# Two-layer hybrid decoder trunk on one core: the mixer's input and output projections as plain fp32 products instead of three split products

## The chip, the cores and the metric

The kernel runs on one core of one Trainium2 chip. The metric is the device time of one execution in microseconds (us); lower is better. The engines named below are TensorE (PE, with its weight loads listed apart as PEld), VectorE (DVE), ScalarE (ACT), GpSimd (POOL) and SyncE (SP), which only issues transfers.

## The reference

The input is one sequence of 256 tokens with 1024 channels. Each of two layers is FFN, mixer, FFN, every one of them behind a modulated LayerNorm and followed by a residual LayerNorm. Cut to what matters:

```python
for l in range(2):
    x = norm(ALPHA * x + 0.5 * gate * swiglu(modulate(x), w_gate, w_up, w_down))   # 1024 -> 2816 -> 1024
    h = modulate(x)
    z = h @ w_in[l]                                   # 1024 -> 2048
    q, k, v, u_ssm, u_pool = split(z, 512, 512, 512, 256, 256)
    y = concat(dilated_attention(q, k, v),            # 8 heads x 64, three branches
               s5(u_ssm),                             # 16 groups, 64 complex states each, scan, GLU
               pool_mixer(u_pool))                    # trailing means of 2, 4, 8, 16
    x = norm(ALPHA * x + gate * (y @ w_out[l]))       # 1024 -> 1024
    x = norm(ALPHA * x + 0.5 * gate * swiglu(modulate(x), ...))
```

All of it is in fp32.

## The kernel before

The 256 tokens are two tiles of 128, called tt 0 and tt 1. Weights come from memory in pieces of 128 x 1024 (512 KB). `process` (L368) loads a piece into a slot called `raw`; for the pieces of the four matrices (`gu` and `wd` of the FFN, `win` and `wout` of the mixer) ACT copies it to `hi` in the type fp32r (L379) and DVE takes the rest, `lo = raw - hi` (L380). So a piece lives on in two slots of the 41 that there are for everything of this size (`N_W`). The other operand is split in the same way: `HT` holds the transposed modulated tokens as hi and lo halves (`parts`, L502).

A product of two split numbers is then three fp32r matmuls, x_hi w_hi, x_lo w_hi and x_hi w_lo. `linear` (L535) does it for the FFN's first matrix and for the mixer's input projection: for each of 8 slices kt of 128 input channels, the three matmuls L544, L545 and L546, each 128x512. The input projection has four parts of 512 columns, named B (the channels of SSM and pooling), V, Q and K; their results are `pB`, `pV`, `pQ`, `pK`. `project` (L549) does it for the FFN's last matrix and the output projection, with two column halves, so six matmuls for each kt (L556, L561); the mixer's accumulators are `dm`.

Inside `mixer` (L822) the steps are written in the list `MIXER_ORDER`. `ssm jj tt` is a chain through a PE product (`pbu`, L914), DVE multiplications (L927, L929), additions on POOL or DVE (L932), scans on DVE (L939), and a PE product into `py` (L950). `scores tt` makes the logits on PE in `psc` (L969), DVE adds the bias into `lg` (L975), DVE takes maxima, ACT the exponentials; `attend` turns the probabilities on PE (`ppt`, L993) and multiplies with V (`po`, L1004). Scores of tt 1 are made in two sets of heads, and the first bank of the second set is the first bank of the first one (`SCORE_BANKS`). `glu` and `pooling` end the other two branches. All three write their results into `HT` again, as hi and lo, each through one ACT and one DVE instruction (L508 and L509, L1033 and L1034, L1072 and L1073). `out` (L1077) multiplies them with `wout`, first tt 0, then tt 1. `chain` (L511) is the residual sum and the two LayerNorms, on DVE almost alone (from `y`, L522, to `z`, L471); the transposes of `z` on PE are `pn` (L475), and ACT makes the modulated `h` (L481).

The order on each engine is not that in which the code is written: every step is recorded with its engine and a written cost, and `Plan.order` (L134) places the steps one after the other by those costs, by slot and bank, and by rank in the program. A step's cost of 0.695 is given for the three matmuls of `linear`. So a change of costs or of steps gives another order on all five engines.

Of the kernel before, what the change touches and what calls it, by code (L numbers as in the profile page):

```python
# [21 lines left out]
NU = DFF // 256  # L22
# [28 lines left out]
WAIT = {"DVE": 0.25, "ACT": 0.25, "Pool": 1.3}  # L51
BUFS = {"w": N_W, "th": 2, "a": 2, "aT": 2, "st": 3, "carry": 1, "a3": 1, "gu": 2, "t": 2, "d0": 1, "d1": 1, "d2": 1, "d3": 1}
# [212 lines left out]
class Build:  # L265
    def __init__(self, tc, io, pools):
        self.tc, self.nc, self.io, self.pools = tc, tc.nc, io, pools
        self.plan = Plan()
        self.items, self.next = [], 0
        self.ready, self.acc, self.bc = {}, {}, {}  # L270
        self.exd, self.turns = [], []
# [96 lines left out]
    def process(self):  # L368

        nc = self.nc  # L370
        x = self.items[self.next]
        self.next += 1
        t = self.slot("raw")
        self.load(lambda: nc.sync.dma_start(out=t[:], in_=self.src(x)), [], [t], 0.5)
        if x[0] == "ada" and x[3] == 0:
            self.start_sum(*x[1:3])
        if x[0] in ("gu", "wd", "win", "wout"):
            hi, lo = self.slot("hi", F32R), self.slot("lo", F32R)
            self.act(1024, lambda: nc.scalar.copy(out=hi[:], in_=t[:]), [t], [hi])  # L379
# [77 lines left out]
    def modulated(self, tt, l, sub):  # L457

        for h, pt in enumerate(self.normed(tt, ("t", "t"))):
            hs = self.slot("h") if h == 0 else hs  # L460
            for k in range(4 * h, 4 * h + 4):
                self.shifted(hs, pt, k, tt, l, sub)
            self.parts(lambda h=h, hs=hs: hs[:, h * 512:(h + 1) * 512].rearrange("p (k t) -> p k t", k=4), [(hs, 4 * h + b) for b in range(4)], 4 * h, 4, tt)
# [20 lines left out]
    def first(self):  # L484

        pts = [list(self.normed(tt, ("t", "t") if tt == 0 else ("d2", "d3"))) for tt in range(2)]
        hs = [self.slot("h") for _ in range(2)]
        for k in range(8):
# [46 lines left out]
    def linear(self, out, tt, pieces):  # L535

        nc = self.nc
        for kt in range(8):
            hi, lo = self.need(pieces[kt // 2])
# [7 lines left out]
            self.pe(0.695, go, [hi, lo] + [(self.HT, (p, kt, tt)) for p in range(2)], [out])  # L547

# [41 lines left out]
    def unit(self, l, sub, f, tt, u, d):  # L590
# [9 lines left out]
        t = self.buf("aT", [128, 2, 2, 128], F32R)  # L600
        self.act(256, lambda: nc.scalar.copy(out=t[:, 0], in_=pt[:]), [pt], [(t, 0)])  # L601
        self.dve(256, lambda: nc.vector.tensor_tensor(out=t[:, 1], in0=pt[:], in1=t[:, 0].bitcast(F32), op=ALU.subtract), [pt, (t, 0)], [(t, 1)])  # L602

        def down():
            for kk in range(2):
                w = self.need(("wd", l, f, u, kk))
                self.project(d, lambda kk=kk: t[:, 0, kk, :], lambda kk=kk: t[:, 1, kk, :], [t], w, u == 0 and kk == 0, u == NU - 1 and kk == 1)
# [214 lines left out]
    def mixer(self, l):  # L822
# [17 lines left out]

        V = lambda: made["v"][:].rearrange("p (s c) -> p s c", s=2)
# [145 lines left out]
        def attend(tt):  # L987
# [20 lines left out]
            self.turned(lambda k: qf()[:, tt, k * 128:(k + 1) * 128], [(place("qf"), ("f", tt))], 4, 0, tt)  # L1008

        def glu(tt):  # L1010
# [20 lines left out]
            self.dve(256, lambda: nc.vector.scalar_tensor_tensor(out=z[:], in0=z[:], scalar=1.0, in1=yv[:], op0=ALU.add, op1=ALU.mult), [z, yv], [z])  # L1031
            kh, kl = [[(HT, (p, kt, tt)) for kt in (4, 5)] for p in range(2)]
# [6 lines left out]
        def pooling(tt):  # L1039
# [29 lines left out]
            for j in range(2):  # L1069
                o = O_PS + l * 2 + j  # L1070
                kh, kl = [[(HT, (p, 6 + j, tt))] for p in range(2)]
                self.act(128, lambda j=j, o=o: nc.scalar.activation(out=HT[:, 0, 6 + j, c], in_=pz[:, j, :], func=AF.Copy, scale=sm[:, o:o + 1]), [pz, sm], kh, 0.1)  # L1072
                self.dve(128, lambda j=j, o=o: nc.vector.scalar_tensor_tensor(out=HT[:, 1, 6 + j, c], in0=pz[:, j, :], scalar=sm[:, o:o + 1],  # L1073
# [3 lines left out]
        def out(tt):  # L1077
            d = [self.bank(f"d{2 * tt + h}", name=f"dm{tt}{h}") for h in range(2)]
            for kt in WOUT:
                xh, xl = (lambda i=i, kt=kt: HT[:, i, kt, cols[tt]] for i in range(2))  # L1080
# [25 lines left out]
def build(tc, io):  # L1106
    with tc.tile_pool(name="sb", bufs=1) as sb, tc.tile_pool(name="ps", bufs=1, space=bass.MemoryType.PSUM) as ps, \
            tc.tile_pool(name="dram", bufs=1, space=bass.MemoryType.DRAM) as dram:
        with tc.manual_schedule():
            Build(tc, io, dict(sb=sb, ps=ps, dram=dram)).run()  # L1110

# [89 lines left out]
```

## Time and profile before

| what | value |
|---|---|
| device time, median of 3 | 1108.52 us (1105.32 to 1110.19) |
| the profiled execution, device time | 1107.35 us |
| its span, from the first instruction to the last | 1105.6 us |
| PE busy | 1026.4 us (93%) |
| DVE busy | 864.6 us (78%) |
| ACT busy | 501.0 us (45%) |
| POOL busy | 300.3 us (27%) |
| mean granted TensorE clock | 0.975 of full speed |

Matmuls are pipelined, so the time of one is read from start to start and not from its length; the busy share says only how long no gap stood between them. The first mixer lies at about 236 to 366 us, the second at about 772 to 895 us, and the four FFNs around them.

### The profile page before, as it was taken

How to read it: one execution, taken by the hardware profiler on the slowest of the kernel's cores; microseconds unless marked ns; L12 is line 12 of the kernel's file. 1: busy time of each engine (PE TensorE's matmuls, PEld its weight loads, DVE VectorE, ACT ScalarE, POOL GpSimd, SP SyncE). 2: the span in 40 equal slices, each digit the busy share in tenths (PEclk: the TensorE clock that was granted, in tenths of full speed). 3: DMA queues.
4: the chain of work that ended last, by engine and by line, in shares of the span. 5: the costliest groups of instructions: out<-in, count | busy, mean ns of one | idle time of the engine just before them, and what ended most of it. 6: DMA issues, size and time to landing. Idle time of an engine off the chain costs nothing. (4 is left out here: it accounts for less than half of the span.)

```text
span 1105.6 us, 13448 instructions
## 1 busy us (share of the span) xinstructions
PE 1026.4 (93%) x4626; PEld 802.6 (73%) x4626; DVE 864.6 (78%) x1254; ACT 501.0 (45%) x799; POOL 300.3 (27%) x449
## 2 busy tenths in 40 slices
PE   4899999979989799999999999999997989999996
PEld 3578877657767577788876887778775767887885
DVE  7978877998899899845389988758987999755423
ACT  3764444253356635434274544415425665544400
POOL 2057758023751100088610000001485010000000
PEclk9899999998998899999999999999998999999998
DMA  9988889984635489946486998968563447765601
GB/s 357 408 340 298 298 300 340 341 307 166 192 115 172 175 309 351 321 131 222 170 299 217 382 342 300 315 207 286 184 220 131 153 171 261 257 204 161 199 3 38
DMA packets 73551, 266.49 MB, mean 241 GB/s; under 512 B 8307, under 2 KB 8443, under 8 KB 73484
## 3 DMA queue, kind: packets, MB, share of 16 engines
q1 hardware_dynamic: 68556, 248.15, 63.5%
q0 software_dynamic: 4928, 17.50, 4.6%
q8 instruction: 36, 0.59, 0.2%
q14 instruction: 31, 0.25, 0.1%
HBM read 258.00 MB, written 7.61 MB: 240 GB/s over the span
## 5 line engine op out<-in xcount | busy, mean ns | idle before, releaser
L379 ACT CAST hi<-raw 128x1024 fp32r<-128x1024 f32 x312 | 323.0, 1052 | 205.2 <-DMA raw<-in_gu_dram 92.6
L380 DVE TENSOR_TENSOR lo<-raw,hi 128x1024 fp32r<-128x1024 f32 x312 | 379.7, 1237 | 42.0 <-ACT hi L379 38.2
L544 PE MATMUL gu<-hi,HT 128*128 128x512 f32 x704 | 291.2, 414 | 10.2 <-ACT hi L379 5.6
L546 PE MATMUL gu<-lo,HT 128*128 128x512 f32 x704 | 281.4, 400 | 8.5 <-DVE lo L380 8.5
L545 PE MATMUL gu<-hi,HT 128*128 128x512 f32 x704 | 283.7, 403 | 0.7 <-DVE HT L509 0.7
L556 PE MATMUL d<-hi,aT 128*128 128x512 f32 x672 | 183.5, 394 | 1.9 <-ACT aT L601 1.7
L546 PEld LDWEIGHTS gu<-lo,HT 128*128 128x128 f32 x704 | 134.2, 191 | 46.6 <-DVE lo L380 14.5
L544 PEld LDWEIGHTS gu<-hi,HT 128*128 128x128 f32 x704 | 134.4, 191 | 42.6 <-ACT hi L379 7.9
L545 PEld LDWEIGHTS gu<-hi,HT 128*128 128x128 f32 x704 | 134.8, 192 | 29.7 <-DVE HT L509 1.6
L556 PEld LDWEIGHTS d<-hi,aT 128*128 128x128 f32 x672 | 125.1, 188 | 33.4 <-ACT aT L601 3.6
L441 POOL TENSOR_TENSOR st<-st,power 128x1 f32<-128x1 f32 x24 | 27.9, 1160 | 385.6 <-DVE st L440 385.6
L388 DVE CUSTOM_DVE_ANT_0 raw<-raw,row,sm 128x1024 f32<-128x1024 f32 x96 | 123.3, 1295 | 3.6 <-DMA raw<-in_at_dram 3.6
L597 DVE TENSOR_TENSOR a<-th,gu 128x256 f32<-128x256 f32 x88 | 36.8, 419 | 99.4 <-ACT th L596 99.2
L596 ACT ACTIVATE th<-gu 128x256 f32<-128x256 f32 x88 | 33.7, 383 | 177.1 <-PE gu L546 176.9
L556 PE MATMUL d<-lo,aT 128*128 128x512 f32 x336 | 104.7, 393 | 0.0
L556 PEld LDWEIGHTS d<-lo,aT 128*128 128x128 f32 x336 | 63.1, 188 | 13.9
L932 POOL TENSOR_TENSOR w<-w 128x256 f32<-128x256 f32 x57 | 53.0, 945 | 50.8 <-DVE w L929 27.7
L395 DVE SCALAR_TENSOR_TENSOR acc<-raw,cond,acc 128x1024 f32<-128x1024 f32 x48 | 63.1, 1315 | 1.3 <-DMA raw<-in_ada_dram 1.3
L602 DVE TENSOR_TENSOR aT<-pa,aT 128x256 fp32r<-128x256 f32 x88 | 37.1, 421 | 33.8 <-ACT aT L601 33.1
L601 ACT CAST aT<-pa 128x256 fp32r<-128x256 f32 x88 | 32.9, 373 | 56.8 <-PE pa L599 56.5
L481 ACT ACTIVATE h<-pn,mod 128x128 f32<-128x128 f32 x96 | 36.8, 466 | 44.8 <-PE pn L475 24.9
L828 POOL DMA_DIRECT2D ex<-exd x2 | 1.1, 561 | 166.2 <-DMA raw<-in_gb_dram 149.5
(206 smaller groups left out, 1219.7 us busy)
## 6 DMA issues: line engine op xcount, KB each, us to landing
raw<-in_gu_dram SPq DMA_DIRECT2D x176, 512.0 KB, 5.3
raw<-in_at_dram SPq DMA_DIRECT2D x96, 512.0 KB, 6.2
raw<-in_wd_dram SPq DMA_DIRECT2D x88, 512.0 KB, 5.6
raw<-in_ada_dram SPq DMA_DIRECT2D x48, 512.0 KB, 5.3
raw<-in_win_dram SPq DMA_DIRECT2D x32, 512.0 KB, 6.3
raw<-in_wout_dram SPq DMA_DIRECT2D x16, 512.0 KB, 4.2
raw<-in_gb_dram SPq DMA_DIRECT2D x12, 512.0 KB, 5.5
lg<-biasd POOLq DMA_DIRECT2D x6, 512.0 KB, 5.8
```

Of the source, the lines that this page charges most:

```text
L379: self.act(1024, lambda: nc.scalar.copy(out=hi[:], in_=t[:]), [t], [hi])
L380: self.dve(1024, lambda: nc.vector.tensor_tensor(out=lo[:], in0=t[:], in1=hi[:].bitcast(F32), op=ALU.subtract), [t, hi], [lo])
L388: self.dve(1090, lambda: nc.vector.tensor_tensor_reduce(out=t[:], in0=t[:], in1=self.row[:], scale=1.0, scalar=self.sm[:, O_ADA + k:O_ADA ...
L395: self.dve(1090, lambda: nc.vector.scalar_tensor_tensor(out=acc[:], in0=t[:], scalar=self.cond[:, q:q + 1], in1=acc[:], op0=ALU.mult, op1= ...
L481: self.act(128, lambda: self.nc.scalar.activation(out=hs[:, k * 128:(k + 1) * 128], in_=pt[:, k % 4, :], func=AF.Identity, scale=sc(), bia ...
L544: nc.tensor.matmul(out[:], xh, hi[:, c], start=kt == 0, stop=False)
L545: nc.tensor.matmul(out[:], xl, hi[:, c], start=False, stop=False)
L546: nc.tensor.matmul(out[:], xh, lo[:, c], start=False, stop=kt == 7)
L556: nc.tensor.matmul(d[h][:], a(), b[:, c[h]], start=start, stop=stop)
L597: self.dve(256, lambda: nc.vector.tensor_tensor(out=a[:], in0=th[:], in1=ps[:, 256:512], op=ALU.mult), [th, ps], [a])
L602: self.dve(256, lambda: nc.vector.tensor_tensor(out=t[:, 1], in0=pt[:], in1=t[:, 0].bitcast(F32), op=ALU.subtract), [pt, (t, 0)], [(t, 1)])
L932: self.either(256, lambda eng, r=r, op=op: eng.tensor_tensor(out=x()[:, :, r, :], in0=x()[:, :, r, :], in1=y()[:, :, r, :], op=op), [kx, k ...
```

## The change

The names in `WHOLE` tell which products are made whole. For all four parts of `win` and for `wout`, a piece is no longer split: the slot `raw` itself is an operand. `linear` takes for these the unsplit `h` (kept in `self.hs`) and one fp32 matmul per kt; `out` takes a new slot `o0` or `o1`, into which attention, GLU and pooling write their results unsplit by ACT, and two fp32 matmuls per kt (`whole_product`). `WHOLE_UNITS` is empty, so the FFNs keep their split products, and `modulated` still splits `h` into `HT` ahead of the mixer too.

```diff
+WHOLE = ("B", "V", "Q", "K", "O")
+WHOLE_UNITS = ()
...
-        if x[0] in ("gu", "wd", "win", "wout"):
+        if whole(x):
+            self.ready[x] = t
+        elif x[0] in ("gu", "wd", "win", "wout"):
             hi, lo = self.slot("hi", F32R), self.slot("lo", F32R)
...
         for kt in range(8):
+            if whole(pieces[kt // 2]):
+                w, hs = self.need(pieces[kt // 2]), self.hs[tt]
+                self.pe(0.86, lambda kt=kt, w=w, hs=hs: nc.tensor.matmul(
+                    out[:], hs[:, kt * 128:(kt + 1) * 128], w[:, kt % 2 * 512:kt % 2 * 512 + 512], start=kt == 0, stop=kt == 7), [w, (hs, kt)], [out])
+                continue
             hi, lo = self.need(pieces[kt // 2])
...
+    def whole_product(self, d, x, key, w, first, last):
+        for h in range(2):
+            self.pe(0.86, lambda h=h: self.nc.tensor.matmul(d[h][:], x(), w[:, h * 512:(h + 1) * 512], start=first, stop=last), key + [w], [d[h]])
...
+        mix = lambda tt: made[f"o{tt}"][:].rearrange("p (k t) -> p k t", k=8)
...
-            self.turned(lambda k: qf()[:, tt, k * 128:(k + 1) * 128], [(place("qf"), ("f", tt))], 4, 0, tt)
+            if whole(("wout", l, 0)):
+                turn(lambda: qf()[:, tt, :], [(place("qf"), ("f", tt))], [lambda: mix(tt)[:, 0:4, :]], [(place(f"o{tt}"), 0)])
...
+            if whole(("wout", l, 4)):
+                self.act(256, lambda: nc.scalar.activation(out=mix(tt)[:, 4:6, :], in_=z[:], func=AF.Copy, scale=0.5), [z], [(place(f"o{tt}"), 1)])
+                return
...
+                if whole(("wout", l, 6)):
+                    self.act(128, lambda j=j, i=i: nc.scalar.activation(out=mix(tt)[:, 6 + j, :], in_=pz[:, j, :], func=AF.Copy, scale=sm[:, i:i + 1]),
+                             [pz, sm], [(place(f"o{tt}"), 2)], 0.1)
+                    continue
...
             for kt in WOUT:
+                if whole(("wout", l, kt)):
+                    w = self.need(("wout", l, kt))
+                    self.whole_product(d, lambda kt=kt: mix(tt)[:, kt, :], [(place(f"o{tt}"), 0 if kt < 4 else kt // 2 - 1)], w, kt == WOUT[0], kt == WOUT[-1])
+                    continue
...
+def whole(x):
+
+    return x[0] == "win" and x[2] in WHOLE or x[0] == "wout" and "O" in WHOLE or x[0] in ("gu", "wd") and x[3] in WHOLE_UNITS
```

The order moves on every engine. Line numbers of the changed kernel are a few to thirty higher (L547 is the whole product of `linear`, L562 that of `out`, L888 and L893 the turn and its copy, L938 `pbu`, L480 `pn`). First, PE at the start of the first mixer, where tt 0 is ready and tt 1 is still in `chain`. Before:

```order
L544 MATMUL pB_2134<-hi_2004,HT 128x512
L545 MATMUL pB_2134<-hi_2004,HT 128x512
L546 MATMUL pB_2134<-lo_2181,HT 128x512
L544 MATMUL pB_2134<-hi_2004,HT 128x512
L545 MATMUL pB_2134<-hi_2004,HT 128x512
L546 MATMUL pB_2134<-lo_2181,HT 128x512
L475 MATMUL pn_2195<-ident,z_2187 128x128 x4
L475 MATMUL pn_2201<-ident,z_2187 128x128 x4
L544 MATMUL pB_2134<-hi_2024,HT 128x512
```

In the changed kernel, from the first product of the mixer:

```order
L547 MATMUL pB_2113<-raw_1937,h_2107 128x512 x2
L547 MATMUL pB_2113<-raw_1958,h_2107 128x512 x2
L547 MATMUL pB_2113<-raw_1982,h_2107 128x512 x2
L547 MATMUL pB_2113<-raw_1991,h_2107 128x512 x2
L547 MATMUL pV_2151<-raw_2037,h_2107 128x512
L888 MATMUL ptr_2158<-ident,bt_2153 128x128 x4
L547 MATMUL pV_2151<-raw_2037,h_2107 128x512
L938 MATMUL pbu_2170<-uu_2164,ex_1877 128x128 x4
L547 MATMUL pV_2151<-raw_2051,h_2107 128x512 x2
L547 MATMUL pV_2151<-raw_2077,h_2107 128x512 x2
L547 MATMUL pV_2151<-raw_2090,h_2107 128x512
L480 MATMUL pn_2200<-ident,z_2197 128x128 x4
```

Before, 18 matmuls of `pB` stand ahead of the transposes of tt 1; now all 8 products of B and 7 of V do, with the first SSM product among them.

Second, DVE in the first mixer, at the scores of tt 1, of which `psc_2841` (before) and `psc_2645` (now) are the first set's first bank. Before:

```order
L939 SCALAR_TENSOR_TENSOR w_367_2804<-rad,carry_2333,w_367_2804 128x128
L939 SCALAR_TENSOR_TENSOR w_369_2742<-rad,carry_2333,w_369_2742 128x128
L927 TENSOR_TENSOR w_368_2876<-w_367_2804,cos_2456 128x512
L929 TENSOR_TENSOR w_368_2876<-w_367_2804,sin_2474 128x2x128
L939 SCALAR_TENSOR_TENSOR w_369_2742<-rad,carry_2333,w_369_2742 128x128
L929 TENSOR_TENSOR w_368_2876<-w_367_2804,sin_2474 128x2x128
L927 TENSOR_TENSOR w_370_2881<-w_369_2742,cos_2456 128x512
L975 TENSOR_TENSOR lg_2318<-psc_2841,lg_2318 128x2x256
```

In the changed kernel:

```order
L951 TENSOR_TENSOR w_338_2609<-pbu_2589,cos_2246 128x512
L1058 SCALAR_TENSOR_TENSOR z_2623<-z_2623,yv_2448 128x256
L956 TENSOR_TENSOR w_334_2618<-w_334_2618 128x2x128
L999 TENSOR_TENSOR lg_2098<-psc_2645,lg_2098 128x2x256
L963 SCALAR_TENSOR_TENSOR w_336_2595<-rad,carry_2233,w_336_2595 128x128
L963 SCALAR_TENSOR_TENSOR w_338_2609<-rad,carry_2233,w_338_2609 128x128
```

Before, the addition into `lg` that frees the bank stands behind the scans (L939) of the last two SSM steps; now it stands ahead of them (L963).

Third, PE at the end of the first mixer, where `out` of tt 1 goes over into the next FFN. Before:

```order
L561 MATMUL dm_7_3084<-lo_3022,HT 128x512
L561 MATMUL dm_3_3085<-hi_2829,HT 128x512 x2
L561 MATMUL dm_3_3085<-lo_3022,HT 128x512
L475 MATMUL pn_3183<-ident,z_3180 128x128 x4
L475 MATMUL pn_3191<-ident,z_3180 128x128 x4
L544 MATMUL gu_3215<-hi_2993,HT 128x512
```

In the changed kernel:

```order
L480 MATMUL pn_2902<-ident,z_2896 128x128 x4
L480 MATMUL pn_2909<-ident,z_2896 128x128 x4
L562 MATMUL dm_3_2852<-raw_2385,o_342_2832 128x512
L562 MATMUL dm_7_2846<-raw_2395,o_342_2832 128x512
L562 MATMUL dm_3_2852<-raw_2395,o_342_2832 128x512
L555 MATMUL gu_2935<-hi_2585,HT 128x512
```

Before, the transposes of tt 0 stand behind the last output product; now three products stand between them and the FFN's first matmul. The second and the third place read alike in the changed kernel's second mixer.

## Rows read from the trace of the kernel before

**Rows 1.** The page: span, busy time and share of PE.

```profile
span 1105.6 us, 13448 instructions
...
PE 1026.4 (93%) x4626; PEld 802.6 (73%) x4626; DVE 864.6 (78%) x1254; ACT 501.0 (45%) x799; POOL 300.3 (27%) x449
```

**Rows 2.** Waits of PE, first mixer: who waited for whom, sum, times, longest.

```profile
PE pB L546 <- DVE lo L380: 6.8, 1, 6.8
PE psc L969 <- DVE lg L975: 5.5, 1, 5.5
PE pB L544 <- ACT HT L508: 1.3, 1, 1.3
```

**Rows 3.** Waits of PE, 355 to 385 us: first mixer into FFN.

```profile
PE gu L546 <- DVE lo L380: 2.5, 1, 2.5
PE gu L544 <- ACT HT L508: 2.0, 1, 2.0
```

**Rows 4.** Waits of PE, second mixer.

```profile
PE psc L969 <- DVE lg L975: 3.0, 1, 3.0
PE ppt L993 <- ACT k L869: 1.7, 1, 1.7
```

**Rows 5.** Waits of PE, 895 to 920 us: second mixer into FFN.

```profile
PE gu L544 <- ACT HT L508: 2.1, 1, 2.1
PE pn L475 <- DVE z L471: 1.3, 1, 1.3
```

**Rows 6.** Windows: stretch, length, busy time of each engine, granted clock, DMA.

```profile
250.00:256.00 6.00, 6.00 (x18) 5.05 (x19) 5.16 (x7) 3.08 (x9) 0.31 (x1) 0.50 0.00 0
333.00:337.00 4.00, 4.00 (x23) 2.88 (x24) 4.00 (x8) 1.74 (x6) 1.57 (x2) 0.50 0.54 178
378.00:386.00 8.00, 7.26 (x23) 5.26 (x24) 7.74 (x11) 6.38 (x15) 0.22 (x1) 0.57 0.21 67
844.00:852.00 8.00, 7.80 (x40) 5.85 (x40) 6.92 (x14) 2.99 (x5) 2.51 (x3) 0.63 0.56 187
856.00:860.00 4.00, 3.08 (x14) 2.16 (x15) 4.00 (x10) 0.42 (x1) 1.44 (x2) 0.60 0.22 50
902.00:905.00 3.00, 3.00 (x9) 2.32 (x9) 2.85 (x3) 1.33 (x2) 0.00 (x0) 0.57 0.33 86
```

**Rows 7.** Timeline of PE, one split product to the next: start, length.

```profile
264.80 0.40 PE L544 MATMUL pV<-hi,HT 128*128 128x512 f32 x1
...
265.50 0.40 PE L544 MATMUL pV<-hi,HT 128*128 128x512 f32 x1
```

**Rows 8.** Timeline and source line of L724 (two plain fp32 products per row).

```profile
76.25 1.88 PE L724 MATMUL pflip<-rev,onehot 128*128 128x512 f32 x4
...
L724 PE MATMUL pflip<-rev,onehot x8: 592/593/697, 76.3 to 80.7; 128*128 128x512 f32 x8
```

**Rows 9.** The page's groups of the two splitting lines.

```profile
L379 ACT CAST hi<-raw 128x1024 fp32r<-128x1024 f32 x312 | 323.0, 1052 | 205.2 <-DMA raw<-in_gu_dram 92.6
L380 DVE TENSOR_TENSOR lo<-raw,hi 128x1024 fp32r<-128x1024 f32 x312 | 379.7, 1237 | 42.0 <-ACT hi L379 38.2
```

**Rows 10.** Windows of L380 alone on DVE: length, busy time, clock, DMA.

```profile
262.00:312.00 50.00, 11.93 (x9) 1.00 0.62 208
312.00:338.00 26.00, 0.00 (x0) 0.87 0.37 122
835.00:862.00 27.00, 0.00 (x0) 0.81 0.40 134
```

**Rows 11.** Timeline of DVE, `chain` from `y` to `z`: tt 1, then tt 0.

```profile
238.07 0.68 DVE L522 SCALAR_TENSOR_TENSOR y<-d,bc 128x512 f32<-128x512 f32 x1
...
250.34 1.00 DVE L471 TENSOR_SCALAR z<-X,st 128x512 f32<-128x512 f32 x2 [0.45 <-POOL st L441]
...
353.51 1.39 DVE L522 SCALAR_TENSOR_TENSOR y<-dm,bc 128x512 f32<-128x512 f32 x2 [0.59 <-PE dm L561]
...
366.20 0.99 DVE L471 TENSOR_SCALAR z<-X,st 128x512 f32<-128x512 f32 x2
```

More of the change, by code (lines that the diff above doesn't have):

```diff
@@ L269, in __init__ @@
         self.items, self.next = [], 0
-        self.ready, self.acc, self.bc = {}, {}, {}
+        self.ready, self.acc, self.bc, self.hs = {}, {}, {}, [None, None]
         self.exd, self.turns = [], []
@@ L459, in modulated @@
         for h, pt in enumerate(self.normed(tt, ("t", "t"))):
-            hs = self.slot("h") if h == 0 else hs
+            if h == 0:
+                hs = self.hs[tt] = self.slot("h")
             for k in range(4 * h, 4 * h + 4):
@@ L487, in first @@
         hs = [self.slot("h") for _ in range(2)]
+        self.hs = list(hs)
         for k in range(8):
@@ L599, in unit @@
         self.pe(0.22, lambda: [nc.tensor.transpose(pt[:, b, :], a[:, b * 128:(b + 1) * 128], self.ident[:]) for b in range(2)], [a, self.ident], [pt])
-        t = self.buf("aT", [128, 2, 2, 128], F32R)
-        self.act(256, lambda: nc.scalar.copy(out=t[:, 0], in_=pt[:]), [pt], [(t, 0)])
-        self.dve(256, lambda: nc.vector.tensor_tensor(out=t[:, 1], in0=pt[:], in1=t[:, 0].bitcast(F32), op=ALU.subtract), [pt, (t, 0)], [(t, 1)])
+        if whole(("wd", l, f, u, 0)):
+            t = self.buf("aT", [128, 2, 128])
+            self.act(256, lambda: nc.scalar.copy(out=t[:], in_=pt[:]), [pt], [t])
+        else:
+            t = self.buf("aT", [128, 2, 2, 128], F32R)
+            self.act(256, lambda: nc.scalar.copy(out=t[:, 0], in_=pt[:]), [pt], [(t, 0)])
+            self.dve(256, lambda: nc.vector.tensor_tensor(out=t[:, 1], in0=pt[:], in1=t[:, 0].bitcast(F32), op=ALU.subtract), [pt, (t, 0)], [(t, 1)])
         def down():
@@ L606, in down @@
                 w = self.need(("wd", l, f, u, kk))
-                self.project(d, lambda kk=kk: t[:, 0, kk, :], lambda kk=kk: t[:, 1, kk, :], [t], w, u == 0 and kk == 0, u == NU - 1 and kk == 1)
+                first, last = u == 0 and kk == 0, u == NU - 1 and kk == 1
+                if whole(("wd", l, f, u, kk)):
+                    self.whole_product(d, lambda kk=kk: t[:, kk, :], [t], w, first, last)
+                else:
+                    self.project(d, lambda kk=kk: t[:, 0, kk, :], lambda kk=kk: t[:, 1, kk, :], [t], w, first, last)
         return down
@@ L1007, in attend @@
                      [p, (dn, (0, tt))], [(place("qf"), ("f", tt))])
-            self.turned(lambda k: qf()[:, tt, k * 128:(k + 1) * 128], [(place("qf"), ("f", tt))], 4, 0, tt)
+            if whole(("wout", l, 0)):
+                turn(lambda: qf()[:, tt, :], [(place("qf"), ("f", tt))], [lambda: mix(tt)[:, 0:4, :]], [(place(f"o{tt}"), 0)])
+            else:
+                self.turned(lambda k: qf()[:, tt, k * 128:(k + 1) * 128], [(place("qf"), ("f", tt))], 4, 0, tt)
         def glu(tt):
@@ L1069, in pooling @@
             for j in range(2):
-                o = O_PS + l * 2 + j
+                i = O_PS + l * 2 + j
+                if whole(("wout", l, 6)):
+                    self.act(128, lambda j=j, i=i: nc.scalar.activation(out=mix(tt)[:, 6 + j, :], in_=pz[:, j, :], func=AF.Copy, scale=sm[:, i:i + 1]),
+                             [pz, sm], [(place(f"o{tt}"), 2)], 0.1)
+                    continue
                 kh, kl = [[(HT, (p, 6 + j, tt))] for p in range(2)]
-                self.act(128, lambda j=j, o=o: nc.scalar.activation(out=HT[:, 0, 6 + j, c], in_=pz[:, j, :], func=AF.Copy, scale=sm[:, o:o + 1]), [pz, sm], kh, 0.1)
-                self.dve(128, lambda j=j, o=o: nc.vector.scalar_tensor_tensor(out=HT[:, 1, 6 + j, c], in0=pz[:, j, :], scalar=sm[:, o:o + 1],
+                self.act(128, lambda j=j, i=i: nc.scalar.activation(out=HT[:, 0, 6 + j, c], in_=pz[:, j, :], func=AF.Copy, scale=sm[:, i:i + 1]), [pz, sm], kh, 0.1)
+                self.dve(128, lambda j=j, i=i: nc.vector.scalar_tensor_tensor(out=HT[:, 1, 6 + j, c], in0=pz[:, j, :], scalar=sm[:, i:i + 1],
                                                                               in1=HT[:, 0, 6 + j, c].bitcast(F32), op0=ALU.mult, op1=ALU.subtract),
```

## The prediction

> **What bounds the kernel now.** I read the page first: PE is busy for 1026.4 of 1105.6 us, DVE for 864.6 [rows 1]. So PE sets the time unless it waits, and what the change is worth follows from two things: how much longer PE's own work gets, and how much of PE's waiting goes away. The second I read from the list of PE's waits, cut to the stretches around the two mixers, since the change touches nothing else. In the first mixer two waits stand out: 6.8 us for the low half of a weight piece at the start, 5.5 us for the addition of the bias to the scores [rows 2]. Going over into the FFN, PE waits 2.5 us for a low half and 2.0 us for the split tokens [rows 3]. The second mixer has 3.0 us at the scores and 1.7 us at the turned probabilities [rows 4], and 2.1 and 1.3 us behind it [rows 5].
>
> A wait costs more than its length. In the six windows of [rows 6] PE is busy nearly throughout, but the granted clock is 0.50 to 0.63 of full speed, that is wholly or partly at 1.2 instead of 2.4 GHz; each of the first four lies right behind one of those waits. Busy time at a granted clock c loses a share 1 - c: 3.0 us in 250 to 256, 2.0 us in 333 to 337, 3.1 us in 378 to 386 (0.43 of 7.26), 2.9 us in 844 to 852 (0.37 of 7.80), 1.2 us in 856 to 860 (0.40 of 3.08) and 1.3 us in 902 to 905.
>
> The base of the sum is the profiled execution's own 1107.35 us, which is its span and 1.75 us around it, and 1.2 us below the median of 1108.52.
>
> **PE's work, added.** A split product (three matmuls) takes 0.70 us, from 264.80 to 265.50 [rows 7]. The plain fp32 product of the same shape is in the trace already: the row of L724 holds two products, listed as four records of 0.593 us that take 1.88 us together, so they start (1.88 - 0.593) / 3 = 0.43 us apart, and a product is two records, 0.86 us [rows 8]. The clock there is the full one, as in rows 7; at half speed the distance would be twice that. The input projection has 2 layers x 4 parts x 2 token tiles x 8 slices = 128 such products: 128 x (0.86 - 0.70) = 20.5 us. The output projection has 2 x 2 x 8 = 32 pairs; six matmuls at 0.70 / 3 are 1.40 us, two whole products 1.72 us: 32 x 0.32 = 10.2 us. Together 30.7 us more, 15.35 us in each layer, all of it on the engine that sets the time.
>
> A rule prices this higher. The Trainium skill, "FP8 and Floating Point Precision", section "TensorE Precision Notes", counts four passes for a true fp32 product; with a pass at the 0.233 us of a split matmul, the estimate from that is 0.93 us for a product and 44.8 us for the change. The trace has the product itself at 0.86 us, so the row decides.
>
> **Work removed.** 48 pieces are split no more: 48 x 1.052 = 50.5 us of ACT and 48 x 1.237 = 59.4 us of DVE [rows 9], half of each per layer, and the low halves of the heads' results with it. None of this lies on PE, so it is worth what it takes out of PE's waits, and these I go through by place.
>
> At the start of the first mixer PE holds pB until a low half comes, 6.8 us, behind tt 1's chain on DVE. That chain lasts from 238.07 to 250.34, 12.3 us [rows 11]. There is no low half any more, and in the new order PE has 15 products of tt 0 before it needs tt 1, 15 x 0.86 = 12.9 us: enough to cover the chain. I take all of it, 6.8 + 3.0 of clock = 9.8 us. The 1.3 us for the first tokens I leave as they are, since ACT must still make `h`.
>
> At the scores of tt 1 the second set waits until DVE has emptied a bank. DVE splits no weight in this stretch, 0.00 us in 312 to 338 and in 835 to 862 [rows 10], so here nothing is removed from DVE's queue; what helps is that the 50 us before are lighter by up to 11.9 us of splits [rows 10], so the SSM steps start earlier, and that the addition now stands ahead of the last scans instead of behind them. I take the wait and its clock: 5.5 + 2.0 = 7.5 us in the first mixer; 3.0 + 1.7 + 2.9 + 1.2 = 8.8 us in the second.
>
> Behind the mixers PE waits for tt 0's chain. It lasts from 353.51 to 366.20, 12.7 us [rows 11]; before, it was covered by 8 pairs of output products of tt 1, 11.2 us, now by 13 of 16 whole products (11.2 us) with three more (2.6 us) behind the transposes to cover ACT and DVE. The FFN's first weights find DVE with 24 x 1.237 = 29.7 us less behind it in the layer. I take 2.5 + 2.0 + 3.1 = 7.6 us in the first layer and 2.1 + 1.3 + 1.3 = 4.7 us in the second.
>
> The waits taken sum to 9.8 + 7.5 + 8.8 + 7.6 + 4.7 = 38.4 us. Some of it comes back, since PE now reaches the SSM's last products and the turned results while DVE, POOL and ACT still work on them. The trace of before does not have these waits. Their bounds are nothing, and the 16.3 us of both score waits; the nearest row is the 1.7 us that PE waits for ACT in the second mixer [rows 4], and I take it once in each layer, 3.4 us.
>
> Other edits are costed at nothing. Attention's result is now copied once by ACT instead of being split by ACT and DVE, so it comes no later. The dead split of `h` ahead of the mixer stays on ACT and DVE, beside PE's products; it would cost its length if DVE's chain were late again. Transfers are the same in number and size, and a piece now holds one slot instead of two, so none starts later for want of a slot.
>
> The sum: 1107.35 + 30.7 - 38.4 + 3.4 = 1103.05, or **1103.1 us**, 0.5% below the median. It is a small difference of two large terms, and both have to be seen in the profile.
>
> **The rivals.** *The score waits stay.* The place is the second set of scores, where DVE has no split to lose and the chain through DVE scans and POOL additions is as long as before. If PE still reaches it as early as DVE is late, 16.3 us are not recovered (and the 3.4 us are in them): 1103.1 + 16.3 - 3.4 = 1116.0 us, slower than before. It decides as soon as the waits recovered in both layers fall below the 30.7 us paid; against it speaks that PE comes there later by 0.16 us for each of the layer's 64 input products, 10 us, and DVE earlier.
>
> *Price and waits cancel.* Half of the score waits stay, or the next FFN still waits for its tokens: about 8 us less recovered than taken, 1108 to 1111 us, no change that can be told.
>
> *DVE's relief reaches further.* The FFNs have small waits for low halves and `a` too; nothing comes back at the scores, and a few of these go as well: 1103.1 - 3.4 - 5 = about 1095 us. Against it: the FFNs behind the mixer keep all their own splits, and DVE works there as before.
>
> *The product is cheaper than the row.* If one record of 0.43 us were all that a whole product needs, the products would give 128 x (0.43 - 0.70) + 32 x (0.86 - 1.40) = -51.8 us instead of +30.7 us, 1103.1 - 82.5 = 1020.6 us if every wait goes as taken. The row speaks against it: two products stand as four records there. Such a rule is in the Trainium skill, "Perfetto Trace Analysis", section "Engine Utilization": fp32 in its low-high form runs at half the output rate. By that rule the trace agrees for one record, 0.43 us against 0.23 us, but not for a whole product.
>
> **How the numbers follow.** The sum as taken (1098 to 1106 us): 0.43. Cancelled (1106 to 1114): 0.26. The score waits stay (above 1114): 0.15. The relief reaches further (below 1098): 0.14. The cheaper product: 0.02. A measurement here tells about 0.5% from no change, that is 1103.0 and 1114.1 us. The likeliest case lies on both sides of the lower bound: a little over two thirds of it, 0.30, is faster, 0.13 the same. Faster 0.30 + 0.14 + 0.02 = 0.46; same 0.13 + 0.26 = 0.39; slower 0.15. The likeliest case's own range is 1098 to 1106 us. For 8 in 10 the range runs from 1093 to 1116 us: it holds the sum, the cancelled case and the edges of the two on either side.
>
> **What the changed kernel's profile would show.** The products right: records of the whole products about 0.43 us apart, and PE's work in each mixer longer by some 15 us. The start right: no wait of several us between the first product of B and the transposes of tt 1, and a full granted clock through it. The scores right: the wait of PE for `lg` under 2 us in both layers; if it is 3 us or more, the first rival has it. The way into the FFN right: no wait over 1 us for tokens or low halves behind `out`. Wrong would be the prediction if whole products stood further apart than 0.43 us, or if PE waited in the mixer for `raw` to land, which no row shows now.

## The result, and the profile after

The changed kernel takes 1096.04 us (median of 4 runs, 1095.10 to 1099.22) against 1106.95 us of the kernel before on the same chip: a ratio of 0.9915, 95% interval 0.9889 to 0.9940. That is faster by 0.6 to 1.1%, more than the 0.5% that a measurement here can tell. The forecast was 1103.1 us, in a range of 1093 to 1116.

The page of the kernel after answers [rows 1]: PE is busy longer, in a shorter span. Behind it the two lines that answer [rows 9]: 264 splits instead of 312 on each engine.

```profile
span 1094.0 us, 12913 instructions
...
PE 1039.4 (95%) x4434; PEld 761.8 (70%) x4434; DVE 803.2 (73%) x1193; ACT 454.6 (42%) x751; POOL 289.7 (26%) x446
...
L384 DVE TENSOR_TENSOR lo<-raw,hi 128x1024 fp32r<-128x1024 f32 x264 | 320.4, 1231 | 45.6 <-ACT hi L383 42.8
L383 ACT CAST hi<-raw 128x1024 fp32r<-128x1024 f32 x264 | 273.0, 1051 | 157.4 <-DMA raw<-in_gu_dram 71.2
```

**The price.** PE's timeline has long rows of whole products (start, length, records); the answer to [rows 7, 8]:

```profile
291.24 5.32 PE L547 MATMUL pK<-raw,h 128*128 128x512 f32 x12
...
347.83 8.32 PE L562 MATMUL dm<-raw,o 128*128 128x512 f32 x19
```

A record lasts 0.592 us, so they start (5.32 - 0.592) / 11 = 0.430 us and (8.32 - 0.592) / 18 = 0.429 us apart. Two records are a product (L547 has 256 records for its 128 products), so a product takes 0.86 us, as the row of L724 had it.

**PE's waits** over the whole span after (who waited for whom, sum, times, longest), the answer to [rows 2 to 5]:

```profile
PE pa L614 <- DVE a L612: 12.3, 12, 3.9
PE pn L480 <- DVE z L476: 11.0, 1, 11.0
PE gu L555 <- ACT hi L383: 5.9, 4, 2.8
PE gu L557 <- DVE lo L384: 4.9, 5, 1.2
PE d L571 <- ACT aT L620: 3.3, 3, 2.3
PE pa L614 <- DVE lo L384: 2.3, 2, 1.2
PE pg L1052 <- ACT o L893: 1.3, 2, 0.7
```

No wait for `lg` or at `pB` is left: in the mixers only the last line stands, 0.7 us in each. The 11.0 us of `pn` is the program's start, which the kernel before has too. New are the longest of the first line, 3.9 us, the longest of the fifth, 2.3 us, and the sixth line.

**The clock**, by windows (length, busy time of PE, PEld, DVE, ACT and POOL, granted clock, DMA), where [rows 6] had 0.50 to 0.63:

```profile
236.00:256.00 20.00, 19.89 (x64) 9.73 (x63) 16.07 (x28) 9.23 (x23) 8.41 (x12) 1.00 0.99 377
316.00:336.00 20.00, 20.00 (x91) 10.77 (x90) 19.49 (x36) 12.31 (x31) 8.03 (x9) 1.00 0.31 106
356.00:372.00 16.00, 15.77 (x68) 11.62 (x67) 12.69 (x20) 10.81 (x18) 2.03 (x2) 1.00 0.51 191
752.00:760.00 8.00, 5.24 (x16) 3.81 (x17) 3.32 (x4) 0.37 (x1) 0.00 (x0) 0.79 1.03 409
840.00:860.00 20.00, 20.00 (x91) 10.80 (x90) 19.43 (x35) 12.94 (x31) 7.18 (x8) 1.00 0.26 89
896.00:908.00 12.00, 10.01 (x40) 7.51 (x39) 11.10 (x13) 7.70 (x16) 0.00 (x0) 0.86 0.38 133
932.00:940.00 8.00, 5.67 (x18) 4.11 (x17) 5.69 (x6) 3.32 (x4) 0.00 (x0) 0.79 0.54 183
```

The first mixer's start, both score places and the first way into the FFN run at the full clock. The other three rows are below it, and they lie outside the mixers' products: one just ahead of the second mixer, two in the last FFN.

**Where the time went.** The FFNs do the same products in both kernels, so the start of the same FFN matmul can be compared. I count the matmuls into `gu` from the start of the program; there are 2112 in both. Numbers 485 and 705 lie ahead of and behind the first mixer with its way into the FFN, 1541 and 1761 those of the second; I call what lies between such a pair the mixer's stretch. PE's timeline of the kernel before:

```profile
215.04 0.39 PE L545 MATMUL gu<-hi,HT 128*128 128x512 f32 x1
...
440.00 0.39 PE L546 MATMUL gu<-lo,HT 128*128 128x512 f32 x1
...
752.05 0.40 PE L545 MATMUL gu<-hi,HT 128*128 128x512 f32 x1
...
963.98 0.39 PE L546 MATMUL gu<-lo,HT 128*128 128x512 f32 x1
```

The same four of the kernel after:

```profile
213.67 0.40 PE L556 MATMUL gu<-hi,HT 128*128 128x512 f32 x1
...
424.46 0.39 PE L557 MATMUL gu<-lo,HT 128*128 128x512 f32 x1
...
734.46 0.40 PE L556 MATMUL gu<-hi,HT 128*128 128x512 f32 x1
...
951.97 0.39 PE L557 MATMUL gu<-lo,HT 128*128 128x512 f32 x1
```

The first mixer's stretch goes from 225.0 to 210.8 us, the second's from 211.9 to 217.5: the whole gain is in the first layer, and the second layer is slower than before. The FFNs between them take 312.1 and 310.0 us.

**What fills the mixers**, by windows that reach from about the first product of B to the next FFN. Before:

```profile
239.00:370.00 131.00, 114.14 (x597) 89.25 (x597) 117.80 (x188) 62.00 (x123) 53.84 (x68) 0.93 0.53 177
772.00:899.00 127.00, 115.04 (x598) 87.35 (x597) 113.33 (x183) 62.15 (x120) 54.44 (x70) 0.96 0.54 184
```

And after:

```profile
237.00:359.00 122.00, 121.33 (x499) 66.84 (x498) 91.31 (x160) 48.32 (x110) 46.68 (x63) 1.00 0.53 190
757.00:882.00 125.00, 124.33 (x514) 69.48 (x512) 92.29 (x161) 47.01 (x105) 45.54 (x62) 1.00 0.49 173
```

Before, DVE (the third busy time) is busy for about 90% of a mixer, longer than PE in the first; the change takes 26.5 us from DVE there (117.80 - 91.31) and PE now works for 99% of it.

The same for the two whole stretches, before and then after:

```profile
215.04:440.00 224.96, 202.79 (x976) 158.38 (x974) 206.52 (x307) 110.69 (x196) 60.22 (x74) 0.95 0.64 228
752.05:963.98 211.93, 197.99 (x961) 152.90 (x960) 186.45 (x273) 110.82 (x195) 61.46 (x76) 0.97 0.60 208
...
213.67:424.46 210.79, 207.78 (x879) 134.99 (x878) 174.71 (x277) 87.32 (x172) 56.81 (x73) 1.00 0.66 244
734.46:951.97 217.51, 207.78 (x866) 134.88 (x865) 158.01 (x245) 88.62 (x172) 54.57 (x72) 0.98 0.57 202
```

PE's idle time (length less busy time) goes from 22.2 to 3.0 us in the first stretch and from 13.9 to 9.7 us in the second.

### The profile page after: what moved, and what is told of

The parts are those of the page before. It is cut to its first block, busy times and chain, and to the rows that moved or that the text cites. A ratio compares the mean times of both kernels' runs of the same rounds, so it can differ in the third digit from the quotient of the medians.

```text
span 1094.0 us, 12913 instructions
## 1 busy us (share of the span) xinstructions
PE 1039.4 (95%) x4434; PEld 761.8 (70%) x4434; DVE 803.2 (73%) x1193; ACT 454.6 (42%) x751; POOL 289.7 (26%) x446
## 4 chain that ended last, share of the span: by engine, by line
PE 77%; DVE 9%; DMA 8%; ACT 3%; issue 2%; SPq 0%; POOLq 0%; POOL 0%; DVEq 0%; ACTq 0%
PE d L571 18%; PE gu L556 12%; PE gu L555 12%; PE gu L557 12%; PE dm L562 4%; DMA raw<-in_gu_dram 3%; DVE lo L384 3%; DMA raw<-in_wd_dram 3%; PE pB L547 3%; PE pQ L547 3%; PE pV L547 3%; PE pK L547 3%; DVE raw L392 2%; PE pa L614 2%; PE pbu L938 1%
## 5 line engine op out<-in xcount | busy, mean ns | idle before, releaser
L384 DVE TENSOR_TENSOR lo<-raw,hi 128x1024 fp32r<-128x1024 f32 x264 | 320.4, 1231 | 45.6 <-ACT hi L383 42.8
L383 ACT CAST hi<-raw 128x1024 fp32r<-128x1024 f32 x264 | 273.0, 1051 | 157.4 <-DMA raw<-in_gu_dram 71.2
L571 PE MATMUL d<-hi,aT 128*128 128x512 f32 x672 | 187.9, 401 | 3.4 <-ACT aT L620 3.3
L445 POOL TENSOR_TENSOR st<-st,power 128x1 f32<-128x1 f32 x24 | 30.3, 1261 | 373.2 <-DVE st L444 373.2
L956 POOL TENSOR_TENSOR w<-w 128x256 f32<-128x256 f32 x54 | 44.7, 850 | 65.2 <-DVE w L953 24.0
L562 PE MATMUL dm<-raw,o 128*128 128x512 f32 x128 | 58.1, 596 | 0.0
```

Source lines behind the costliest of these rows:

```text
L562: self.pe(0.86, lambda h=h: self.nc.tensor.matmul(d[h][:], x(), w[:, h * 512:(h + 1) * 512], start=first, stop=last), key + [w], [d[h]])
L571: nc.tensor.matmul(d[h][:], a(), b[:, c[h]], start=start, stop=stop)
L956: self.either(256, lambda eng, r=r, op=op: eng.tensor_tensor(out=x()[:, :, r, :], in0=x()[:, :, r, :], in1=y()[:, :, r, :], op=op), [kx, k ...
```

## The experiments

Two theories stood against each other. *Relief*: the waits went because DVE and ACT have fewer splits. *Cover*: they went because PE's products last longer and stand in another order, whatever DVE does. Each ratio compares a kernel with the kernel before, run on the same chip (its medians there are 1104.82 to 1106.95 us, so the ratios compare better than the medians); the mixers' stretches are taken from one profiled execution each, between the same four `gu` matmuls as above, and need not be typical: e5's execution took 3.8 us more than its median, e9's 2.4 us less. "Recovered" is what the stretch lost against the kernel before, plus the price of the whole products in it (0.16 us for each input product, 0.32 us for each output pair).

| kernel | median, us | ratio, 95% interval | mixer 1 | mixer 2 | recovered 1 | recovered 2 |
|---|---|---|---|---|---|---|
| before | 1106.95 | | 225.0 | 211.9 | | |
| the change | 1096.04 | 0.9889 to 0.9940 | 210.8 | 217.5 | 29.6 | 9.8 |
| e1 splits kept | 1105.28 | 0.9983 to 1.0023 | 221.9 | 211.4 | 18.5 | 15.9 |
| e2 input only | 1095.23 | 0.9869 to 0.9913 | 212.1 | 211.1 | 23.1 | 11.0 |
| e3 output only | 1089.03 | 0.9820 to 0.9861 | 215.8 | 202.0 | 14.3 | 15.0 |
| e4 no dead split | 1095.99 | 0.9883 to 0.9935 | 212.1 | 215.3 | 28.3 | 12.0 |
| e5 addition first | 1108.06 | 0.9996 to 1.0042 | 229.8 | 210.7 | -4.8 | 1.2 |
| e6 early zeroing | 1098.19 | 0.9907 to 0.9956 | 210.5 | 212.8 | 29.9 | 14.5 |
| e7 O, and B of layer 1 | 1082.36 | 0.9771 to 0.9834 | 209.5 | 201.5 | 23.2 | 15.5 |
| e8 O, and B, V, Q, K of layer 1 | 1085.24 | 0.9791 to 0.9846 | 212.6 | 203.7 | 27.8 | 13.3 |
| e9 late pieces | 1093.32 | 0.9846 to 0.9896 | 210.9 | 209.4 | 29.5 | 17.9 |
| e10 output only, splits kept | 1104.32 | 0.9955 to 0.9998 | 222.3 | 209.4 | 7.8 | 7.6 |
| e11 O, and B, V of layer 1 | 1084.05 | 0.9758 to 0.9820 | 208.1 | 201.6 | 27.1 | 15.4 |
| e12 B of layer 1 alone | 1105.32 | 0.9961 to 1.0000 | 221.0 | 214.5 | 6.6 | -2.6 |

The FFNs between the mixers take 309.7 to 313.1 us in these executions, and from the fourth matmul to the last one 125.2 to 126.3 us: differences of 2 or 3 us in a row of this table tell nothing. Each edit also puts the steps of all five engines in a new order, so a small difference need not come from what the edit is about.

### e1: the splits kept

```diff
 if whole(x):
     self.ready[x] = t
+    hi, lo = self.slot("hi", F32R), self.slot("lo", F32R)
+    self.act(1024, lambda: nc.scalar.copy(out=hi[:], in_=t[:]), [t], [hi])
+    self.dve(1024, lambda: nc.vector.tensor_tensor(out=lo[:], in0=t[:], in1=hi[:].bitcast(F32), op=ALU.subtract), [t, hi], [lo])
```

> The changed kernel with the 48 pieces still copied by ACT and subtracted by DVE into two slots that nobody reads; the products stay whole. Theory relief (the waits went because DVE and ACT lost 24 x 1.237 and 24 x 1.052 us of splits in each layer): the waits at the scores and behind the mixers come back, the start stays covered, so 1096 plus up to 16.3 + 12.3 us, between 1106 and 1124 us, with PE waiting several us for the addition to the scores or for the next FFN's low halves. Theory cover (PE no longer waits for low halves and its longer products cover the chains, whatever DVE does beside): 1095 to 1101 us, no wait of 3 us in either mixer.

The gain is gone: 1105.28 us, 0.7 us below relief's range and far from cover's. But the waits came back only in part as relief said. The waits of PE from 355 to 390 us (the way into the FFN) are back:

```profile
PE gu L560 <- DVE lo L387: 4.1, 1, 4.1
PE gu L558 <- ACT HT L517: 2.0, 1, 2.0
```

The waits at the scores are not (no wait of PE for `lg` is listed), and the second mixer's stretch, 211.4 us, is shorter than the change's 217.5 and near the 209.4 us that the change has there without its late piece (e9, below). So in the full change the relief is worth 11 us in the first layer, at the way into the FFN above all, and next to nothing in the second. The edit also takes up the slots again that the change had freed; but in the first stretch no wait of DVE for a transfer or for `hi` is listed, in e1 or in e10 below, so it is DVE's own work, and not room for pieces, that makes PE wait there.

### e2 and e3: one projection at a time

```diff
-WHOLE = ("B", "V", "Q", "K", "O")
+WHOLE = ("B", "V", "Q", "K")      # e2
+WHOLE = ("O",)                    # e3
```

> Only the input projection whole, the output projection split as before. Theory that the terms add up place by place: the price of 20.5 us is paid, the waits at the start and at the scores are gone (-26.1), those behind the mixers (12.3 us) stay: 1107 + 20.5 - 26.1 = 1101 to 1104 us. Rival, the two projections relieve the same waits: without the output's 10.2 us of price the time falls below the full change, to 1086 to 1094 us, because the waits behind the mixer go with the input's splits alone.

> Only the output projection whole, the input projection split as before. Place by place: 10.2 us of price, the waits behind the mixers gone (-12.3), those at the start and at the scores stay: 1103 to 1107 us. Rival, the two relieve the same waits (the input's splits no longer have the output's behind them): below 1100 us, with the waits at the scores smaller than 5.5 and 3.0 us.

Both lie on the rival's side, e2 1 us above its range. The output projection alone takes 1089.03 us, better than the whole change; with it the waits at the scores are gone as well (0.5 us is the longest for `lg`), and the start of the first mixer waits as before. PE's waits from 240 to 256 us in e3:

```profile
PE pB L557 <- DVE lo L384: 6.8, 1, 6.8
```

The input projection alone takes 1095.23 us, as much as the whole change. The parts relieve in part the same waits: in the first layer e2 and e3 recover 23.1 and 14.3 us, together 37.4, and the whole change 29.6; in the second 11.0 and 15.0 against 9.8. Each part pays its own price, and the input's is twice the output's.

### e4: without the dead split

```diff
-            self.parts(lambda h=h, hs=hs: hs[:, h * 512:(h + 1) * 512].rearrange("p (k t) -> p k t", k=4), ...)
+            if sub != 1:
+                self.parts(lambda h=h, hs=hs: hs[:, h * 512:(h + 1) * 512].rearrange("p (k t) -> p k t", k=4), ...)
```

> The changed kernel without the split of the modulated tokens ahead of the mixer, whose halves nobody reads (8 copies on ACT, 8 subtractions on DVE). If it lies beside PE's work, as it was costed: 1093 to 1099 us, the same within 0.3%. Rival, it lies on the way of the tokens at the mixer's start or of DVE's queue behind it: 1086 to 1092 us.

1095.99 us: the dead split costs nothing, as it was costed.

### e5: the addition ahead of the scans, in the kernel before

```diff
 self.dve(512, lambda e=e, v=v, p=p: nc.vector.tensor_tensor(out=v(), in0=p[e][:], in1=v(), op=ALU.add), [p[e]] + keys, keys)
+if tt:
+    self.plan.ops[-1].rank -= 120
```

> The kernel before, no product and no split changed, only the additions of the bias to the scores of tt 1 put ahead in DVE's queue by rank. Theory order (the score waits went because the addition stands ahead of the last scans): the waits of 5.5 and 3.0 us and the slow clock behind them go, 1107 - 16.3 = 1090 to 1095 us, if the SSM steps that are put back by 1 to 2 us do not hold PE. Theory relief (the waits went because DVE and ACT have fewer splits): the wait moves to the SSM's products or the probabilities, 1104 to 1109 us.

No gain (1108.06 us). No wait of PE for `lg` is left, but these stand in its place, in PE's waits from 320 to 350 us and from 850 to 875 us:

```profile
PE py L950 <- POOL w L932: 4.7, 2, 4.2
...
PE pg L1027 <- DVE yt L1025: 4.2, 1, 4.2
```

PE now waits for the SSM's last additions on POOL in the first mixer and for the GLU on DVE in the second. So in the kernel before the place of the addition only decided where PE waited: the branches' work on DVE and POOL ends late, wherever the addition stands.

### e6 and e9: the new wait ahead of the second mixer

In the kernel after, DVE's timeline and PE's (start, length, and in brackets the idle time before it and what ended it) show where the 3.9 us come from. DVE:

```profile
753.09 1.28 DVE L399 SCALAR_TENSOR_TENSOR acc<-raw,cond,acc 128x1024 f32<-128x1024 f32 x1 [4.02 <-DMA raw<-in_ada_dram]
754.29 0.41 DVE L612 TENSOR_TENSOR a<-th,gu 128x256 f32<-128x256 f32 x1
```

PE:

```profile
754.76 0.69 PE L614 MATMUL pa<-ident,a 128*128 128x128 f32 x2 [3.93 <-DVE a L612]
```

DVE's queue holds the accumulation of a piece of `in_ada` ahead of the FFN's last `a`, and the piece comes late. Two edits tried the reason: e6 zeroes the accumulator earlier, since SP had stood still for it; e9 moves the pieces later in the stream.

```diff
-        if x[0] == "ada" and x[3] == 0:
-            self.start_sum(*x[1:3])
+        for y in self.items[max(0, self.next - 1):self.next + 12]:
+            if y[0] == "ada" and y[3] == 0 and (y[1], y[2]) not in self.acc:
+                self.start_sum(*y[1:3])
```

```diff
-SIDE = (..., (((0, 5),), 1, 19), ...)
+SIDE = (..., (((0, 5),), 9, 23), ...)
```

> The changed kernel with the zeroing of an accumulator of the conditioning, and the transfer of its bias row behind it, up to 11 pieces earlier. Theory: the new wait of 3.9 us at 751 to 755 us, with the slow clock behind it, comes from SP's queue, which stood still from 728.3 to 735.1 us until ACT had zeroed the accumulator, so that the piece of in_ada that DVE waits for comes late: without it 1096 - 5.9 = 1089 to 1092 us. Rival: the memory is the bound there (DMA share 1.03 from 750 on), the pieces come no sooner: 1095 to 1097 us with the wait in its place.

> The changed kernel with the eight pieces of in_ada that come in the mixer's stretch of the stream spread over its pieces 9 to 23 instead of 1 to 19, so that on DVE their accumulation stands behind the last unit of the FFN. Theory (the wait of 3.9 us at 751 to 755 us is DVE's queue held by a piece that the full memory delivers late): that wait and its slow clock go, 1096 - 5.9 = 1088 to 1092 us. Rival (the memory is the bound itself): the wait moves to the weight pieces in the mixer and the time stays, 1094 to 1098 us.

e6: 1098.19 us, no gain (1 us above the rival's range), and the wait is still there, from 755 to 770 us, now for `aT`, the next step of the same unit, which stands behind the next accumulation:

```profile
PE d L572 <- DVE aT L622: 3.3, 1, 3.3
```

SP's stop was not the reason: its wait of 6.7 us for the zeroed accumulator is gone in e6. e9: 1093.32 us, between the two ranges, and the stretch in which PE had been busy for 5.24 of 8 us at a clock of 0.79 reads, by windows:

```profile
752.00:760.00 8.00, 8.00 (x32) 5.48 (x31) 4.04 (x6) 0.37 (x1) 0.00 (x0) 1.00 1.03 409
```

The memory is as full as in the kernel after (DMA share 1.03), and PE does not wait: it was DVE's order in front of a full memory. The second mixer's stretch is 8.1 us shorter in the profiled execution. The two ratios' intervals overlap a little, so the 2.7 us between the medians would not show the gain by themselves; that the wait is gone is shown by the rows, and the 8.1 us are one execution against one.

The same wait stands in every other run in which the second layer's input pieces are not split and `in_ada` has its old place (3.9 us in e2, 4.5 us in e4), and in no run that splits these pieces, e1 with its whole products included. So it comes with the pieces that are no longer split; by which step was not tested. A full memory alone is not enough: in the kernel before the DMA share is 1.02 to 1.03 from 762 to 777 us, and no wait of PE is listed there.

### e7, e8 and e11: whole products where PE waits

```diff
-WHOLE = ("B", "V", "Q", "K", "O")
+WHOLE = ("B", "O")                # e7; e8 keeps all five; e11: ("B", "V", "O")
...
-    return x[0] == "win" and x[2] in WHOLE or ...
+    return x[0] == "win" and x[2] in WHOLE and x[1] == 0 or ...
```

> Whole products in the output projection of both layers and in B of the first layer alone. Theory place by place: against the output projection alone (1089.0) this takes away the wait of 6.8 us at the first mixer's start and 3.0 us of slow clock, at a price of 16 x 0.16 = 2.6 us: 1080 to 1084 us. Rival: the start needs V's whole products too as cover, and the wait moves to the transposes of tt 1: 1087 to 1091 us.

> The input projection whole in the first layer only, the output projection whole in both. Theory: in the second layer the whole input products buy nothing (no wait there that the output alone does not remove) and bring the late piece: against the full change 10.2 us of price and 5.9 us of wait less, 1096 - 16.1 = 1078 to 1083 us. Rival: they are needed in both layers, and the second mixer's waits come back: 1088 to 1096 us.

> As the run with O in both layers and B in the first (1082.4 us), with V of the first layer whole too. Theory: the first mixer's waits of pV at 250 to 262 us and their slow clock (some 6 us) go for 16 x 0.16 = 2.6 us: 1078 to 1081 us. Rival: the wait goes over to Q, whose split tokens of tt 1 come no sooner: 1082 to 1086 us.

e7 takes 1082.36 us, the lowest median of all and in the theory's range, 2.0% below the kernel before (1.7 to 2.3%). B in the first layer alone recovers 8.9 us there (23.2 - 14.3), for 2.6 us. e8 takes 1085.24 us, 2 us above the theory's range: without whole input products the second mixer's stretch falls from 217.5 to 203.7 us; the difference holds the price and the late piece. They had bought little there: with the late piece out of the way (e9) the second stretch recovers 17.9 us, without them 13.3 to 15.5 us (e3, e7, e8, e11), 2 to 5 us for a price of 10.2. e11 lies in the rival's range and cannot be told from e7, though not for the rival's reason: from 238 to 300 us no wait of PE above 0.2 us is left, for Q or any other, and the granted clock of the stretch is 0.99 instead of 0.97. V's whole products recover 3.9 us more there (27.1 - 23.2) for 2.6 us, too little a difference to be seen.

In e7's first mixer, by windows, DVE is busy for 103 of 122 us and PE for 119:

```profile
239.00:361.00 122.00, 119.28 (x549) 79.57 (x548) 103.15 (x172) 57.79 (x124) 52.99 (x67) 0.94 0.56 189
```

### e10: the output whole, its splits kept

The edit is that of e1 with `WHOLE = ("O",)`.

> Only the output projection whole, as in the run that took 1089.0 us, but its 16 pieces are still copied by ACT and subtracted by DVE into two slots that nobody reads. If it is these splits (9.9 us of DVE and 8.4 us of ACT in each layer) that the output part's gain comes from: the score waits and those behind the mixers return, 1099 to 1110 us. If it is the heads' results, which have no subtraction in the tail of each branch, and PE's longer products: 1087 to 1092 us.

1104.32 us, 15 us more than e3 (by the ratios 1.4%): the 16 splits that nobody reads take nearly all of the gain back. PE's waits from 355 to 390 us and from 880 to 910 us show where a part of it is:

```profile
PE gu L560 <- DVE lo L387: 1.8, 1, 1.8
PE d L574 <- DVE lo L387: 1.1, 1, 1.1
...
PE d L574 <- DVE lo L387: 2.0, 1, 2.0
PE gu L560 <- DVE lo L387: 1.0, 1, 1.0
```

The waits for `lg` do not come back here either, against what was expected of the splits.

### e12: only the start

`WHOLE = ("B",)`, in the first layer alone.

> B of the first layer alone whole, all else as in the kernel before. By the prediction's term for the start (6.8 us of wait and 3.0 us of clock for 2.6 us of price): 1107 - 7.2 = 1098 to 1102 us. Rival: PE comes earlier to the scores and waits there for what it no longer waits for at the start: 1103 to 1108 us.

1105.32 us, a ratio of 0.998 (0.9961 to 1.0000), the rival's range: not the 7.2 us that the start's term alone gives. The wait of 6.8 us at the start is gone, and PE waits for part of it later, near the scores as the rival had it, but for the SSM's additions on POOL. Its waits from 320 to 345 us and from 835 to 870 us, and the window that holds the first of them:

```profile
PE py L974 <- POOL w L956: 4.0, 3, 2.5
...
PE pg L1052 <- DVE yt L1050: 2.7, 1, 2.7
...
328.00:340.00 12.00, 7.91 (x32) 5.37 (x31) 12.00 (x21) 4.64 (x18) 3.69 (x4) 0.59 0.27 87
```

DVE is busy for all 12 us while PE is busy for 7.91 at a clock of 0.59. The second row lies in the second mixer, whose products are those of before: there the wait for `lg`, 3.0 us before, only stands in another place.

## Why the prediction was right, and where its terms were off

The direction was right, and the time lies in the range, 7 us below the likeliest value. It is outside the likeliest case's own range (1098 to 1106 us) and in that of the rival by which the relief reaches further, which had a chance of 0.14. That rival's reason fits in part: little came back in the mixers, but what the FFNs gained is within the scatter. Step by step:

**The price, 30.7 us: right.** Whole products start 0.43 us a record apart, as the row of L724 had shown, so the sum of 20.5 and 10.2 us stands. The rival of the cheaper product is out. The four passes of the Trainium skill ("FP8 and Floating Point Precision", section "TensorE Precision Notes") would have made it 44.8 us by an estimate; the records of this kernel agree with the lower figure.

**The start, 9.8 us: the wait went, and by the reason given.** tt 1's chain lies beside 15 whole products at a full clock. As a term by itself it was too large: without the rest of the change it recovers 6.6 us (e12), with the output whole 8.9 us (e7 against e3).

**The scores, 7.5 and 8.8 us: gone, but neither reason given is what did it.** The addition's new place on DVE is not enough (e5): PE then waits for POOL and DVE a few us further on. Fewer splits in the 50 us before are not needed: with all weight splits kept the wait does not come back (e1, e10). What is shown is that each of three edits takes it away: the input whole (e2), the output whole (e3), and the whole products with all splits kept (e1, and the output alone in e10). In all of them PE's products last longer, and in all but e2 the heads' results lose their subtractions on DVE; which of the two does it was not tested.

**The ways into the FFN, 7.6 and 4.7 us: mostly right.** The waits for the tokens shrank to 0.4 us each and that of a `gu` product for a low half is gone, and it is relief that did it: with the splits kept the waits for low halves come back there, 4.1 us in e1 and 1.8 in e10. Behind each mixer 1.2 us stand at `pa` for a low half instead, and in the last FFN 2.3 us at `aT`.

**What comes back, 3.4 us: near the size of one wait, but in another place.** In the mixers only 0.7 us each came back. Ahead of the second mixer 3.9 us of wait and a slow clock did, through a piece of `in_ada` in front of DVE's queue (e9), which the prediction had not looked for: it asked only whether a transfer would start later for want of a slot.

**The sum.** It took 23.2 us net of waits in the first layer (9.8 + 7.5 + 7.6 - 1.7) and 11.8 in the second (8.8 + 4.7 - 1.7). The stretches show 29.6 and 9.8 us, together 39.4 instead of 35.0. Another 2.1 us were gained in the FFNs between the mixers and 1.4 us ahead of the first, and 0.4 us lost in the last (within the scatter of such stretches), which with the 4.4 us makes about 7. So the step that was off is the first layer's sum of waits, 6.4 us too small. The windows of the whole stretches show where: PE's idle time fell by 19.2 us (22.2 - 3.0) against 15.1 net taken (6.8 + 5.5 + 2.5 + 2.0 - 1.7), and the other 10.4 us stand against 8.1 us of slow clock. So 4.1 of the 6.4 us are idle time that the short list of waits left out.

**Where luck helped.** The second layer's 9.8 us look close to the 11.8 taken only because the late piece stands against them: with the piece moved (e9) 17.9 us are recovered there. So both layers' waits were worth some 6 us more than taken, and the late piece, which the prediction did not have, hid the second error. The forecast was nearer than its terms.

What the prediction did not see, and what a reader should take from the runs, is that its terms are not separate. In the kernel before a mixer has two long queues, PE's and DVE's, each busy for about 90% of it; taking one of PE's single waits away moves the waiting on (e5, e12). In the first layer the stretch gets shorter as DVE's work does, until PE is full. Its windows in e10, e3 and e7:

```profile
215.32:437.66 222.34, 208.24 (x943) 152.01 (x942) 203.39 (x297) 110.88 (x196) 59.51 (x73) 0.95 0.64 231
...
217.38:433.23 215.85, 202.70 (x943) 149.66 (x942) 195.30 (x291) 102.44 (x187) 58.99 (x74) 0.98 0.66 238
...
216.36:425.85 209.49, 205.20 (x928) 147.42 (x926) 186.72 (x286) 98.41 (x184) 60.76 (x73) 0.97 0.68 245
```

DVE's 206.5 us before, 203.4 in e10, 195.3 in e3 and 186.7 in e7 go with stretches of 225.0, 222.3, 215.8 and 209.5 us; the change takes DVE down to 174.7 us, and the stretch is still 210.8, since PE is busy for 207.8 of it. The whole products cost PE time that is free only while PE would have waited. In the first layer the input's whole products filled such waits; in the second most of their 10.2 us was simply paid (17.9 us recovered in e9 against 15.0 in e3).

## What to carry to other kernels

When two engines are both near 90% in a stretch, add up how long each is busy there: the longer time is a floor for the stretch, and waits of the one for the other are not terms to be added. How far above the floor the stretch lies went here with how near the other engine was: in the first layer 18.4 us before (206.5 us of DVE, 202.8 of PE), 13.1 in e3, 4.3 in e7, 3.0 in the change. Trading work from the second engine for more on the first pays piece by piece, only where the first would have waited: less than half of this change's whole pieces (20 of 48), at the right places, gained more than twice as much as all of them (a ratio of 0.980 against 0.9915). Look also at steps fed by a transfer that stand in an engine's queue ahead of something urgent: here they cost nothing in the kernel before, and 3.9 us of waiting after the change.

## What the runs showed that was not expected

With the memory full from 745 to 765 us (DMA share 1.02 to 1.03, 388 to 411 GB/s), the five pieces of `in_ada` issued from 735 to 760 us in the kernel after took 12.4 us at the median from issue to landing, against 4.2 us for all 48 of them; each is 512 KB. That made an addition of 1.28 us on DVE cost PE 3.9 us and some clock.
